# Splitting the input projection weights once and reloading the halves, in a hybrid decoder step on one core

## The chip, the cores and the metric

One core of one Trainium2 chip runs the whole program. The metric is device time in microseconds (us), the median of several runs. Matmuls run on TensorE (PE in the profile, PEld for its weight loads), elementwise work on VectorE (DVE), ScalarE (ACT) and GpSimd (POOL), and almost all transfers are issued from one queue, that of SyncE (SP), which takes its entries in order.

## The reference, cut to what matters

```python
h = rms_norm(x, norm_g)                                   # 2048 prompt tokens and 8 x 4 sample tokens, D = 1024
(sb_q, sb_k, sb_v, sb_g, pl_u, pl_g, gl_q, gl_k, gl_v, gl_g, gl_r, mg) = \
    jnp.split(h @ w_in, _split_points(), axis=-1)          # 9232 columns
o_a = stick_breaking_attention(q, k_all, v_all, ...) * silu(sb_g)     # 8 heads of 64, causal
o_b = multiscale_pool(u_ext, ...) * silu(pl_g)
o_c = rms_norm(gla_chunked(gl_q, gl_k, gl_v, log_a, s0)) * silu(gl_g) # 4 heads, a recurrence in chunks
merged = gates[0] * (o_a @ w_pa) + gates[1] * (o_b @ w_pb) + gates[2] * (o_c @ w_pc)
y = x + merged @ w_o
```

All of it is float32. The change concerns only how the columns of `w_in` reach TensorE.

## The kernel before

**Products from halves.** A float32 product is made of three matmuls of a rounded format (float32r): each operand is split into a high half (the value rounded) and a low half (the value minus the high half), and `mm3` adds high x high, high x low and low x high. So every weight tile is split on the chip: a cast gives `wh` (L160 on DVE or L162 on ACT), a subtraction gives `wl` (L164 on POOL or DVE).

**Groups, phases, units.** The prompt is cut into four groups of 512 tokens (the first also carries the 32 sample tokens). Phase a takes the groups one after the other: the norm, the projections for attention, pooling and the merge gates, and the attention itself. Phase b takes them again for the gated linear attention, four heads per group. Phase c merges the branches and makes the output projection. The weights come in units of 256 columns, each in two halves of the contracted dimension, [128, 4, 256] each, which is 0.5 MiB as float32. A group uses 24 units of `w_in` in phase a and 12 in phase b, so 72 such tiles, and each group loads and splits all of them anew. Phase c has 96 tiles of the other weights.

**The weight pipeline.** `plan` is the list of all weight tiles in the order of use, with the engines that are to split them: cast on DVE and subtraction on POOL in phase a (`SPA`), cast on ACT and subtraction on POOL or DVE by turns (one on POOL, two on DVE) in phase b (`SPB`). `load_h` (L145 to L151) loads the next raw tile into one of two buffers `wr`; `split_h` splits it into one of four buffers `wh` and one of four `wl`. `take`, called at the start of each unit, splits until four tiles stand ready (this unit's two and the next unit's two), then loads raw tiles until six are under way. So a raw tile is loaded two units before its matmuls and split one unit before them. A buffer comes free when the unit that used it is done on TensorE.

**What sets the order.** Matmuls keep their program order (`keep_in_program_order`). The order on the other engines and on the SP queue is chosen when the program is built, by a scheduler that plays the program against a timeline of its own. In phase a the projections of one group are interleaved with the attention of the same group: `z_step` makes scores (`z`), two sigmoids on ACT (L551, L552), a scan on DVE (`om`, L560), a product (`be`, L565, by turns on DVE and POOL); two steps later `t_step` transposes `be` on TensorE and splits the result (`ah` on ACT, L591; `al` on DVE, L592), and `v_step` multiplies these with the values (`acc`). The number of such steps grows with the group: a head takes 2 steps in the first group and 8 in the fourth. In phase b `mix_head` ends each head with a Newton iteration of tiny DVE instructions (`rstd_newton`, L264 to L269, tile `grt`), a product on DVE (`gate`, L1379) and a transpose on TensorE (`z<-ident,gate`). At the start of each group of phase b `h_load` (L292) brings the group's normalised input back from DRAM, as tiles `hTh` and `hTl` of 0.5 MiB for each 128 tokens.

Of the kernel before, what the change touches and what calls it, by code (L numbers as in the profile page):

```python
# [8 lines left out]
F32 = mybir.dt.float32  # L9
F32R = mybir.dt.float32r  # L10
# [7 lines left out]
P = 128  # L18
T = 2048
TG = 512  # L20
NG = T // TG
# [19 lines left out]
NH, PF, PL = 4, 4, 6  # L41
# [28 lines left out]
def f32(ap):  # L70
    return ap.bitcast(F32)
# [3 lines left out]
def hybrid_step(ctx, tc, x_prompt, x_sample, cache_k, cache_v, state_pool, state_gla, page_table, norm_g, w_in,  # L75
                sb_qnorm_g, sb_knorm_g, sb_bias, pool_w, pool_scale, gla_w2, gla_b2, gla_onorm_g, w_pa, w_pb, w_pc, w_o,
                y_p, y_s, k_p, v_p, pool_p, gla_p, k_s, v_s, pool_s, gla_s, phases="abc"):
    nc = tc.nc
# [17 lines left out]
    dram = ctx.enter_context(tc.tile_pool(name="scratch", bufs=1, space=DRAM))  # L96
    wp = ctx.enter_context(tc.tile_pool(name="wp", bufs=1))
# [42 lines left out]

    plan, loaded, ahead = [], [], []
    count = [0]

    def load_h():
        seg, eh, el = plan.pop(0)  # L145
        raw = wp.tile([P, 4, 256], F32, name="wr", bufs=PL - PF)
        o = 0
        for v, n in seg:
            nc.sync.dma_start(raw[:, :, o:o + n], v)
            o += n  # L150
        loaded.append((seg, raw, eh, el))  # L151

    def split_h():
        if not loaded:
            load_h()
        seg, raw, eh, el = loaded.pop(0)
        wl = wp.tile([P, 4, 256], F32R, name="wl", bufs=NH)
        wh = wp.tile([P, 4, 256], F32R, name="wh", bufs=NH)
        if eh[count[0] % len(eh)] == "v":
            nc.vector.tensor_copy(wh, raw)  # L160
        else:
            nc.scalar.copy(wh, raw)  # L162
        count[0] += 1
        (nc.vector if el[count[0] % len(el)] == "v" else nc.gpsimd).tensor_tensor(wl, raw, f32(wh), op=sub)  # L164
        ahead.append((seg, wh, wl))

    def take(*segs):
        n = len(segs)
        while len(ahead) < min(max(n, PF), len(ahead) + len(loaded) + len(plan)):
            split_h()  # L170
        while plan and len(ahead) + len(loaded) < PL:
            load_h()
        got = [ahead.pop(0) for _ in range(n)]
        for (key, _, _), want in zip(got, segs):
            assert [(str(v), m) for v, m in key] == [(str(v), m) for v, m in want]
        return [w[1] for w in got], [w[2] for w in got]
# [4 lines left out]
    def win_unit(cols):  # L181
        return take(*halves(win, cols))
# [7 lines left out]

    def early(n, e):
        for i in range(n):
            plan[i] = (plan[i][0], *e)

    def plan_b():
        us = []
# [94 lines left out]
        for x in range(2):  # L291
            nc.sync.dma_start(f32(HT[x])[:, :, c0:c1], hd[g][x][:, :, c0:c1])  # L292

    # ------------------------------------------------------------------ norm, attention, pooling
    def phase_a(ctx):
        cst = ctx.enter_context(tc.tile_pool(name="cst_a", bufs=1))
        xpool = ctx.enter_context(tc.tile_pool(name="xpool", bufs=1))
# [10 lines left out]
        gB = cst.tile([P, D], F32, name="gB")  # L308
        nc.sync.dma_start(gB, norm_g.broadcast_to([P, D]))
        load_h()  # L310
        nc.sync.dma_start(x0[1], xp[P:2 * P, :])
        load_h()
# [572 lines left out]
            while step():  # L885
                pass

    # ------------------------------------------------------------------ sample attention over the paged cache
    def sample_attn(ctx, cst):
        R = P  # L890
        idv = ident.rearrange("p (b h q) -> p b h q", b=4, h=H)
# [134 lines left out]
            for c in range(4):  # L1026
                nc.sync.dma_start(od[0][c][:, TG + bt * 16:TG + (bt + 1) * 16], og[:, c, :])

    # ------------------------------------------------------------------ gated linear attention
    def phase_b(ctx):  # L1030
        cst = ctx.enter_context(tc.tile_pool(name="cst_b", bufs=1, reuse_waits="tile"))
        gp = ctx.enter_context(tc.tile_pool(name="gla", bufs=1, reuse_waits="tile"))
# [467 lines left out]
        for _ in sa:  # L1500
            n_sa += 1

    # ------------------------------------------------------------------ gates, branch projections, output
    def phase_c(ctx):
        mq = ctx.enter_context(tc.tile_pool(name="mrq", bufs=1, reuse_waits="tile"))
        on = ctx.enter_context(tc.tile_pool(name="on", bufs=1, reuse_waits="tile"))
# [84 lines left out]

    for ph, make in (("a", plan_a), ("b", plan_b), ("c", plan_c)):
        if ph in phases:
            for _ in range(NG):
                plan += make()
    if "a" in phases:
        with ExitStack() as st:
            pin[0] = PIN
            early(2, EARLY)
            banks(st, "pa", **PSA)  # L1600
            phase_a(st)
            pin[0] = False
# [36 lines left out]
```

## Time and profile before

| What | Value |
|---|---|
| median of 3 runs | 3198.27 us (3193.27 to 3203.49) |
| profiled execution, its span | 3195.0 us (3.3 us under the median; the page gives no other time of it) |
| PE busy | 3030.3 us, 95% |
| DVE, ACT, POOL busy | 2225.0 us (70%), 1350.3 us (42%), 1656.2 us (52%) |
| DMA, SP's queue | 417.13 MB, 42.3% of the 16 engines' span |
| first group of phase a | about 0 to 385 us |
| second, third, fourth group of phase a | about 385 to 760, 760 to 1180, 1180 to 1735 us |
| first group of phase b, the other three | about 1735 to 1955, 1955 to 2560 us |
| rest of the last head, and phase c | 2560 to 3195 us |

The busy share of an engine is the time in which it executes something. A busy PE can still be slower than it could be, since matmuls overlap in the pipeline; and an idle engine costs time only if PE, or another engine that PE waits for, waits for it. So the profile is read stage by stage: how busy each engine is in the stage, what PE waits for, and what the instruction that releases PE was itself held up by.

### The profile page before, as it was taken

The numbers are of one execution on the slowest core, as the hardware profiler recorded it, in microseconds if no ns is written. First come the engines' busy times: TensorE is split into PE (matmuls) and PEld (weight loads), VectorE is DVE, ScalarE is ACT, GpSimd is POOL, SyncE is SP. The second block draws the span as 40 slices with busy tenths as digits, with TensorE's granted clock in tenths as the row PEclk, the third lists the DMA queues.
The fourth block names the chain that finished last, engine by engine and source line by source line (L and its number), as shares of the span: only waits on it lengthen the run. The fifth ranks groups of instructions, "written<-read, shape, count | busy, mean of one in ns | idle before, by whom it ended". The sixth has DMA issues, their size and how long they took to land.

```text
span 3195.0 us, 56555 instructions
## 1 busy us (share of the span) xinstructions
PE 3030.3 (95%) x21874; PEld 2654.1 (83%) x21874; DVE 2225.0 (70%) x3968; ACT 1350.3 (42%) x2483; POOL 1656.2 (52%) x1329
## 2 busy tenths in 40 slices
PE   7999999999999999899999999999999989999999
PEld 7899997778877788777778888788878868988999
DVE  7765479777898889998997677757676664443332
ACT  2222324444355453465555544555445543332221
POOL 4555466655756555555544444554545545354442
PEclk9999999999999999999999999999999989999999
DMA  5433454345343444233334344334334337666553
GB/s 191 141 110 120 135 182 136 119 140 188 113 145 111 137 130 149 86 95 88 98 113 144 86 131 139 115 100 142 107 114 129 115 114 243 224 190 205 176 162 113
DMA packets 400960, 437.52 MB, mean 137 GB/s; under 512 B 25968, under 2 KB 323276, under 8 KB 400428
## 3 DMA queue, kind: packets, MB, share of 16 engines
q1 hardware_dynamic: 395572, 417.13, 42.3%
q0 software_dynamic: 5120, 16.78, 1.7%
q8 instruction: 173, 2.83, 0.4%
q14 instruction: 95, 0.78, 0.1%
HBM read 339.22 MB, written 94.78 MB: 136 GB/s over the span
## 4 chain that ended last, share of the span: by engine, by line
PE 39%; DVE 10%; ACT 3%; issue 2%; POOL 1%; DMA 1%; SPq 0%; ACTq 0%; DVEq 0%; POOLq 0%
PE pj L112 21%; PE z L112 13%; DVE om L560 2%; PE at L112 2%; PE acc L112 1%; DVE lv L1094 1%; DVE be L565 1%; PE z L117 1%; PE at L117 1%; DVE grt L268 1%; DVE al L592 1%; DVE gate L1379 0%; DVE lv L1091 0%; PE acc L117 0%; ACT L1121 0%
## 5 line engine op out<-in xcount | busy, mean ns | idle before, releaser
L164 POOL TENSOR_TENSOR wl<-wr,wh 128x1024 fp32r<-128x1024 f32 x272 | 691.8, 2544 | 440.8 <-ACT wh L162 224.5
L112 PE MATMUL pj<-hTh,wh 128*128 128x512 f32 (+2 forms) x1824 | 670.2, 367 | 17.7 <-DVE ut L738 6.3
L112 PE MATMUL pj<-hTh,wl 128*128 128x512 f32 (+2 forms) x1824 | 635.9, 349 | 0.0
L112 PE MATMUL pj<-hTl,wh 128*128 128x512 f32 (+2 forms) x1824 | 635.8, 349 | 0.0
L112 PE MATMUL pj<-wh,hTh 128*128 128x256 f32 (+1 forms) x1840 | 548.4, 298 | 4.0 <-DMA hTh<-hd 2.6
L112 PE MATMUL pj<-wh,hTl 128*128 128x256 f32 (+1 forms) x1840 | 529.2, 288 | 5.3 <-DVE hTl L402 5.3
L112 PE MATMUL pj<-wl,hTh 128*128 128x256 f32 (+1 forms) x1840 | 530.1, 288 | 0.3 <-POOL wl L164 0.3
L112 PEld LDWEIGHTS pj<-hTh,wh 128*128 128x128 f32 x1824 | 348.9, 191 | 80.2 <-issue 27.9
L112 PEld LDWEIGHTS pj<-hTh,wl 128*128 128x128 f32 x1824 | 347.7, 191 | 44.1
L112 PEld LDWEIGHTS pj<-wh,hTh 128*128 128x128 f32 (+1 forms) x1840 | 356.0, 193 | 19.2 <-issue 8.3
L112 PEld LDWEIGHTS pj<-hTl,wh 128*128 128x128 f32 x1824 | 349.5, 192 | 26.9 <-issue 1.0
L565 POOL TENSOR_TENSOR be<-be,om 128x512 f32<-128x512 f32 (+1 forms) x160 | 176.6, 1103 | 364.6 <-DVE om L560 338.6
L112 PEld LDWEIGHTS pj<-wh,hTl 128*128 128x128 f32 (+1 forms) x1840 | 356.4, 194 | 6.2 <-DVE hTl L402 5.9
L112 PEld LDWEIGHTS pj<-wl,hTh 128*128 128x128 f32 (+1 forms) x1840 | 355.6, 193 | 1.4 <-POOL wl L164 0.5
L560 DVE TENSOR_TENSOR_SCAN om<-om,car 128x512 f32<-128x512 f32 x192 | 325.1, 1700 | 28.6 <-ACT om L552 28.2
L162 ACT CAST wh<-wr 128x1024 fp32r<-128x1024 f32 x194 | 202.7, 1048 | 289.8 <-PE pj L112 126.7
L591 ACT CAST ah<-at 128x512 fp32r<-128x512 f32 (+2 forms) x352 | 161.1, 493 | 330.5 <-PE at L117 197.8
L551 ACT ACTIVATE be<-z,bB 128x512 f32<-128x512 f32 (+2 forms) x320 | 200.4, 626 | 237.1 <-DVE z L548 164.3
L160 DVE CAST wh<-wr 128x1024 fp32r<-128x1024 f32 x190 | 201.9, 1064 | 74.1 <-PE pj L112 50.2
L592 DVE TENSOR_TENSOR al<-at,ah 128x512 fp32r<-128x512 f32 (+2 forms) x352 | 189.1, 560 | 72.8 <-ACT ah L591 71.5
L164 DVE TENSOR_TENSOR wl<-wr,wh 128x1024 fp32r<-128x1024 f32 x112 | 149.0, 1332 | 98.3 <-ACT wh L162 95.0
L552 ACT ACTIVATE om<-z,nbB 128x512 f32<-128x512 f32 (+2 forms) x320 | 200.5, 627 | 0.2 <-DVE be L565 0.2
(521 smaller groups left out, 6712.4 us busy)
## 6 DMA issues: line engine op xcount, KB each, us to landing
wr<-in_w_in_dram SPq DMA_DIRECT2D x224, 512.0 KB
wr<-in_w_in_dram SPq DMA_DIRECT2D x128, 256.0 KB
gt<-gd SPq DMA_DIRECT2D x72, 256.0 KB
gd<-gt SPq DMA_DIRECT2D x70, 256.0 KB
wr<-in_w_pc_dram SPq DMA_DIRECT2D x32, 512.0 KB
wr<-in_w_o_dram SPq DMA_DIRECT2D x32, 512.0 KB
x<-in_x_prompt_dram SPq DMA_DIRECT2D x26, 512.0 KB
vc<-vd SPq DMA_DIRECT2D x48, 256.0 KB
```

Source lines behind the costliest of these rows:

```text
L112: i = nc.tensor.matmul(*a, **k)
L117: i = nc.tensor.transpose(*a, **k)
L160: nc.vector.tensor_copy(wh, raw)
L162: nc.scalar.copy(wh, raw)
L164: (nc.vector if el[count[0] % len(el)] == "v" else nc.gpsimd).tensor_tensor(wl, raw, f32(wh), op=sub)
L268: nc.vector.scalar_tensor_tensor(tr, tr, -0.5, xr, op0=mul, op1=mul)
L551: nc.scalar.activation(be[:, :w], z[:, :w], AF.Sigmoid, bias=bB[:, h:h + 1], scale=0.125)
L552: nc.scalar.activation(om[:, :w], z[:, :w], AF.Sigmoid, bias=nbB[:, h:h + 1], scale=-0.125)
L560: nc.vector.tensor_tensor_scan(ov, ov, ov, init, op0=mul, op1=ALU.min)
L565: (nc.vector if i % 2 == 0 else nc.gpsimd).tensor_tensor(be[:, :w], be[:, :w], om[:, 1:w + 1], op=mul)
L591: nc.scalar.copy(ah[:, jr, tr_], pv[:, jr, tr_])
L592: nc.vector.tensor_tensor(al[:, jr, tr_], pv[:, jr, tr_], f32(ah)[:, jr, tr_], op=sub)
```

## The change

In the first group, a tile of `w_in` is loaded raw and split as before, but both halves go into one tile `w2` of [128, 2, 4, 256] (1 MiB, four buffers, in place of four `wh` and four `wl`), and SP stores that tile to a DRAM tile `wk` of its own. In the three later groups the tile is not loaded raw and not split: one transfer of 1 MiB brings `w2` back from `wk`, ready for the matmuls. `load_h` does this, and `take` starts such a load only when fewer than four tiles stand ready or under way, so it is issued one unit ahead of its use, as soon as the buffer is free. Phase c loads and splits as before. Each plan entry carries a key and the word "keep", "load" or "split".

```diff
     def load_h():
-        seg, eh, el = plan.pop(0)
+        seg, eh, el, key, how = plan.pop(0)
+        if how == "load":
+            w = wp.tile([P, 2, 4, 256], F32R, name="w2", bufs=NH)
+            nc.sync.dma_start(f32(w), kept[key])
+            loaded.append((seg, None, w, None, None, how))
+            return
         raw = wp.tile([P, 4, 256], F32, name="wr", bufs=PL - PF)
...
     def split_h():
         if not loaded:
             load_h()
-        seg, raw, eh, el = loaded.pop(0)
-        wl = wp.tile([P, 4, 256], F32R, name="wl", bufs=NH)
-        wh = wp.tile([P, 4, 256], F32R, name="wh", bufs=NH)
+        seg, raw, eh, el, key, how = loaded.pop(0)
+        if how == "load":
+            ahead.append((seg, eh[:, 0], eh[:, 1]))
+            return
+        w = wp.tile([P, 2, 4, 256], F32R, name="w2", bufs=NH)
+        wh, wl = w[:, 0], w[:, 1]
...
+        if how == "keep":
+            kept[key] = dram.tile([P, 2, 4, 256], F32, name=f"wk{len(kept)}")
+            nc.sync.dma_start(kept[key], f32(w))
         ahead.append((seg, wh, wl))
 
     def take(*segs):
...
-        while plan and len(ahead) + len(loaded) < PL:
+        while plan and len(ahead) + len(loaded) < (PL if plan[0][4] != "load" else PF):
             load_h()
...
-            for _ in range(NG):
-                plan += make()
+            for g in range(NG):
+                how = "split" if ph == "c" else "load" if g else "keep"
+                plan += [(seg, eh, el, (ph, i), how) for i, (seg, eh, el) in enumerate(make())]
```

The order of the matmuls is the same in both programs. What else moves is shown at three places, before and after. Line numbers of the changed kernel are 13 to 14 higher from `split_h` on.

POOL, in the fourth group of phase a, where one attention head ends (`oT`) and the next is prepared (`qd`, `kdu`), before:

```order
L565 TENSOR_TENSOR be<-be,om 128x512
L565 TENSOR_TENSOR be<-be,om 128x256
L587 MEMSET ah 128x128
L588 MEMSET al 128x128
L164 TENSOR_TENSOR wl<-wr,wh 128x1024
L565 TENSOR_TENSOR be<-be,om 128x512
L614 TENSOR_TENSOR oT<-oT,sg 64x512
L474 TENSOR_TENSOR qd<-qr__14549,qd 128x4x64
L164 TENSOR_TENSOR wl<-wr,wh 128x1024
L474 TENSOR_TENSOR kdu<-kr__14834,kdu 128x4x64
```

The same place after:

```order
L578 TENSOR_TENSOR be<-be,om 128x512 x2
L578 TENSOR_TENSOR be<-be,om 128x256
L600 MEMSET ah 128x128
L601 MEMSET al 128x128
L578 TENSOR_TENSOR be<-be,om 128x512
L627 TENSOR_TENSOR oT<-oT,sg 64x512
L487 TENSOR_TENSOR qd<-qr__14145,qd 128x4x64
L487 TENSOR_TENSOR kdu<-kr__14422,kdu 128x4x64
```

The subtractions of the weights are gone and the attention's own work follows without them; on DVE the casts are gone in the same way.

SP's queue, at the first units of phase b (`hTh`, `hTl` is the input of 128 tokens, read from `hd`; `gd`, `od` are stores of phase a's last results), before:

```order
L149 DMA wr<-in_w_in_dram 128x4x256
L778 DMA gd_21_299<-gt 128x512
L149 DMA wr<-in_w_in_dram 128x4x256
L778 DMA gd_22_300<-kr__19423 128x512
L616 DMA od_3_193<-oT 128x512
L292 DMA hTl<-hd_1_71 128x8x128
L292 DMA hTh<-hd_0_70 128x8x128
```

The same place after (`w_18859` is a tile `w2`, `wk_18862` its place in DRAM):

```order
L176 DMA wk_18862<-w_18859 128x2048
L155 DMA wr<-in_w_in_dram 128x4x256
L791 DMA gd_21_299<-gt 128x512
L176 DMA wk_18867<-w_18864 128x2048
L155 DMA wr<-in_w_in_dram 128x4x256
L791 DMA gd_22_300<-kr__18873 128x512
L629 DMA od_3_193<-oT 128x512
L305 DMA hTl<-hd_1_71 128x8x128
L305 DMA hTh<-hd_0_70 128x8x128
```

Two stores of 1 MiB now stand ahead of the loads of the third block of tokens.

SP's queue, in the third group of phase a, after the first four heads' queries, keys (`kr`) and values (`vr`) have been projected, before:

```order
L530 DMA kc<-kd_0_78 128x512
L531 DMA kx<-kd_0_78 64x512
L149 DMA wr<-in_w_in_dram 128x4x256 x2
L791 DMA out_dram<-kr__9202 128x4x256
L794 DMA out_dram<-vr__9411 128x4x256
```

The same place after (`w_9219` and `w_9221` are the two tiles of the first four heads' gate unit, `w_9333` and `w_9335` those of the unit after it, the other four heads' queries):

```order
L543 DMA kc<-kd_0_78 128x512
L544 DMA kx<-kd_0_78 64x512
L149 DMA w_9219<-wk_933 128x2048
L149 DMA w_9221<-wk_938 128x2048
L804 DMA out_dram<-kr__9022 128x4x256
L149 DMA w_9333<-wk_1081 128x2048
L149 DMA w_9335<-wk_1086 128x2048
L807 DMA out_dram<-vr__9223 128x4x256
```

The loads for the queries' unit now stand behind the store of the keys, which waits until the keys are normalised on POOL.

## Rows read from the trace of the kernel before

**Rows 1.** The page: its head, and busy time and share of each engine.

```profile
span 3195.0 us, 56555 instructions
PE 3030.3 (95%) x21874; PEld 2654.1 (83%) x21874; DVE 2225.0 (70%) x3968; ACT 1350.3 (42%) x2483; POOL 1656.2 (52%) x1329
```

**Rows 2.** Windows: stretch, length; PE, PEld, DVE, ACT, POOL busy; clock; DMA; GB/s.

```profile
0.00:385.00 385.00, 352.78 (x2692) 339.84 (x2693) 246.04 (x503) 113.87 (x262) 203.77 (x166) 0.97 0.45 140
385.00:760.00 375.00, 368.31 (x2156) 310.40 (x2156) 284.01 (x475) 147.66 (x300) 225.60 (x164) 1.00 0.45 142
760.00:1180.00 420.00, 406.47 (x2395) 337.98 (x2393) 363.79 (x606) 197.55 (x385) 249.01 (x178) 0.99 0.45 138
1180.00:1735.00 555.00, 515.86 (x3032) 418.88 (x3031) 505.51 (x859) 297.19 (x559) 288.76 (x219) 0.97 0.34 104
1735.00:1955.00 220.00, 200.53 (x1924) 187.87 (x1922) 153.24 (x343) 106.17 (x200) 99.17 (x119) 0.97 0.39 114
1955.00:2560.00 605.00, 567.16 (x5553) 502.09 (x5552) 417.90 (x844) 309.16 (x551) 308.53 (x290) 0.97 0.42 124
```

**Rows 3.** Waits of PE, 1180 to 1735: total us, times, longest.

```profile
PE acc L112 <- DVE al L592: 25.5, 24, 3.2
PE at L117 <- ACT kX L507: 5.1, 6, 1.9
```

**Rows 4.** DVE's groups by form, 1180 to 1735: busy us, mean ns; idle before.

```profile
L560 DVE TENSOR_TENSOR_SCAN om<-om,car 128x512 f32<-128x512 f32 x112 | 179.9, 1610 | 17.3 <-ACT om L552 17.1
L565 DVE TENSOR_TENSOR be<-be,om 128x512 f32<-128x512 f32 x56 | 60.5, 1080 | 0.5
L160 DVE CAST wh<-wr 128x1024 fp32r<-128x1024 f32 x46 | 44.7, 973 | 10.4 <-PE pj L112 5.2 <-DMA wr<-in_w_in_dram 5.1
```

**Rows 5.** Instructions of single lines: ns of the shortest/median/longest (L565, L268: whole span).

```profile
L560 DVE TENSOR_TENSOR_SCAN om<-om,car x112: 1251/1279/4279, 1180.2 to 1731.6; 128x512 f32<-128x512 f32 x112
L592 DVE TENSOR_TENSOR al<-at,ah x156: 275/678/692, 1183.9 to 1727.3; 128x512 fp32r<-128x512 f32 x118, 128x256 fp32r<-128x256 f32 x19, 128x128 fp32r<-128x128 f32 x19
L565 DVE TENSOR_TENSOR be<-be,om x160: 255/681/2714, 114.5 to 1731.0; 128x512 f32<-128x512 f32 x96, 128x128 f32<-128x128 f32 x32, 128x384 f32<-128x384 f32 x32
L268 DVE SCALAR_TENSOR_TENSOR grt<-grt,grx x48: 144/163/2293, 1832.3 to 2630.7; 128x4 f32<-128x4 f32 x48
```

**Rows 6.** Timeline in the fourth group of phase a: start us, length us.

```profile
1470.56 2.52 POOL L164 TENSOR_TENSOR wl<-wr,wh 128x1024 fp32r<-128x1024 f32 x1
...
1470.75 3.42 DVE L560 TENSOR_TENSOR_SCAN om<-om 128x512 f32<-128x512 f32 x1
```

**Rows 7.** Waits of PE, 1955 to 2560.

```profile
PE z L117 <- DVE gate L1379: 13.1, 8, 2.9
PE at L112 <- DVE scx L1324: 8.1, 5, 4.2
```

**Rows 8.** Timeline at the end of a head of phase b.

```profile
2334.95 2.39 POOL L164 TENSOR_TENSOR wl<-wr,wh 128x1024 fp32r<-128x1024 f32 x1 [0.34 <-ACT wh L162]
2335.06 2.29 DVE L268 SCALAR_TENSOR_TENSOR grt<-grt,grx 128x4 f32<-128x4 f32 x1
...
2337.58 1.66 DVE L1379 SCALAR_TENSOR_TENSOR gate<-at,gry,gate 128x256 f32<-128x256 f32 x4
```

**Rows 9.** Windows at the starts of the first two groups of phase b.

```profile
1740.00:1750.00 10.00, 10.00 (x86) 10.00 (x86) 4.12 (x5) 3.88 (x7) 1.28 (x1) 1.00 1.00 287
...
1960.00:1970.00 10.00, 10.00 (x88) 9.46 (x87) 8.78 (x31) 2.88 (x7) 1.29 (x1) 1.00 1.02 307
```

**Rows 10.** The chain of work that ended last: start us, us, what.

```profile
1748.24 7.73 DMA hTh<-hd
```

**Rows 11.** Timeline, third group of phase a: PE and SP's queue.

```profile
818.82 0.40 PE L112 MATMUL pj<-hTh,wh 128*128 128x512 f32 x1
...
825.81 0.38 SPq L791 DMA_DIRECT2D out_dram<-kr__9202  x1
...
829.96 0.28 PE L112 MATMUL pj<-wh,hTh 128*128 128x256 f32 x1
```

More of the change, by code (lines that the diff above doesn't have):

```diff
@@ L142, in hybrid_step @@
     count = [0]
+    kept = {}
     def load_h():
-        seg, eh, el = plan.pop(0)
+        seg, eh, el, key, how = plan.pop(0)
[4 more added lines that the diff above has]
+            return
         raw = wp.tile([P, 4, 256], F32, name="wr", bufs=PL - PF)
@@ L150, in load_h @@
             o += n
-        loaded.append((seg, raw, eh, el))
+        loaded.append((seg, raw, eh, el, key, how))
     def split_h():
@@ L168, in take @@
         n = len(segs)
-        while len(ahead) < min(max(n, PF), len(ahead) + len(loaded) + len(plan)):
+        most = len(ahead) + len(loaded) + len(plan)
+        while len(ahead) < min(max(n, PF), most):
             split_h()
-        while plan and len(ahead) + len(loaded) < PL:
+        while plan and len(ahead) + len(loaded) < (PL if plan[0][4] != "load" else PF):
             load_h()
@@ L192, in early @@
         for i in range(n):
-            plan[i] = (plan[i][0], *e)
+            plan[i] = (plan[i][0], *e, *plan[i][3:])
     def plan_b():
```

## The prediction

> **What bounds the kernel now.** I read the busy shares first: PE is busy 95% of the span [rows 1], so nothing is won except where PE is idle, or runs at the lower of its two clock levels. The windows show where that is. In the three groups that the change relieves, PE is idle 6.7, 13.5 and 39.1 us in phase a and 37.8 us in phase b, 97 us in all (length minus PE busy) [rows 2]. The granted clock there is 1.00, 0.99, 0.97 and 0.97 of 2.4 GHz; a mean of 0.97 is some 6% of the time at 1.2 GHz, so a loss of 3% of the stretch: 0, 4, 17 and 18 us, 39 us in all. These two sums, 97 and 39, are all that the change can win on PE.
>
> Then I asked who makes PE wait. In the fourth group of phase a DVE is busy 505.5 of 555 us, 91% [rows 2], and PE waits above all for DVE's `al`, the split of the attention weights: 25.5 of the 39.1 us [rows 3]. In phase b it waits for `gate` and `scx`, both on DVE, 13.1 and 8.1 us [rows 7]. So the second question is what fills DVE, and the third what stretches its instructions. The scan of 512 columns takes 1.28 us in the median, 1.61 in the mean and 4.28 at most [rows 4, 5]. The timeline shows why: a scan that begins 0.2 us after POOL began to subtract a weight tile runs 3.42 us and ends 1.1 us after POOL does, which is most of a scan's own length [rows 6]. In phase b the same is plainer: a DVE instruction on 4 columns (0.16 us in the median [rows 5]) takes 2.29 us and ends with POOL's subtraction to within 0.01 us; `gate`, for which PE waits, follows 0.2 us later [rows 8]. `al`, whose one input lies in PSUM, is never stretched (678 ns in the median, 692 at most) [rows 5].
>
> **What the change removes.** In each later group 48 tiles of phase a lose a cast on DVE and a subtraction on POOL, and 24 tiles of phase b lose a cast on ACT, and a subtraction on POOL or DVE. None of these is on PE; PE's own matmuls are the same, in the same order.
>
> Fourth group of phase a. The casts are 44.7 us of DVE [rows 4]. Scans give back at most 112 x (1.610 - 1.279) = 37 us and the products `be` 56 x (1.080 - 0.681) = 22 us [rows 4, 5]; POOL's other work stretches them too, so I take 45 of these 59. DVE falls from 505 to about 415 us, 75% of the stretch. With a quarter of its time free it no longer runs late by a whole step, and the projections lie two steps ahead of `al`. I take three quarters of the 39 us idle, 29, and half of the clock's 17, 8: **37 us**. Bounds: 0 and 56.
>
> Second and third group. DVE stands at 76% and 87% already [rows 2]; waits are fewer, and some belong to the start of a group, which the change doesn't touch. Half of the 20 us: **10 us**. Bounds: 0 and 24, with the clock's 4.
>
> Phase b, three groups. A tiny instruction held for 2.29 us in place of 0.16 stands just ahead of `gate` [rows 5, 8]; 12 heads times 2.1 us is 25 us, but not every head is hit, while `scx` and the steps before it gain too. Half of the 37.8 us idle, 19, and a third of the clock's 18, 6: **25 us**. Bounds: 0 and 56.
>
> ACT's casts in phase b I cost at nothing: ACT is busy 51% there [rows 2] and PE's waits in these stretches name it for 5 us only [rows 3]. Sum won: **72 us**, between 0 and 136.
>
> **What it adds.** 72 stores of 1 MiB in the first group, and 216 loads of 1 MiB in place of raw loads of 0.5 MiB. When the DMA engines were busy all the time they moved 287 to 307 GB/s [rows 9]; a pair of tiles, 2.10 MB, then takes 6.8 to 7.3 us. That is my price for a unit's load.
>
> Three places matter, since a load is now issued only when its buffers are free, one unit ahead.
> The usual unit: the third group's gate unit runs from 818.82 to 829.96, 11.1 us, back to back [rows 11]. That is the shortest that a load has; on average it is 1350 / 72 = 18.8 us in phase a and 605 / 36 = 16.8 us in phase b [rows 2]. 7.3 us fit in each: cost 0. The running unit is the cover; were it gone, every unit would cost its 7 us.
> Behind another wait: the next unit's loads are queued behind the store of the keys, which SP issued at 825.81, 4.2 us before that unit's first matmul at 829.96 [rows 11]. If that store comes no earlier, the loads begin at about 826 and PE waits 2.7 to 3.2 us, once in this group and less in the others: I take **3 us**, 0 to 10.
> Start of phase b: the DMA engines are saturated, and PE's input `hTh` lands after 7.73 us on the chain that ended last [rows 9, 10]. Two stores of 1 MiB come ahead of it: 0 to 7.3 us, I take **4**, since they wait for splits that may come after the loads. In the next group the weight loads put 1 MiB more ahead of such loads in a full window: **2 us**, 0 to 3.7.
> Queues: SP has 24 entries more in all (72 + 216 added, 264 raw loads gone), some 0.4 us each [rows 11], beside a queue that waits most of the time: 0. In the first group the stores make 131 GB/s on top of 140 in phase a (50.3 MB in 385 us) [rows 2], 271 together; that is nearly full, but the raw loads behind them are due two units later, and nobody waits for the stores until 360 us later. 0, at most 10. A new wait of SP for PE's last unit holds what stands behind it, attention's `kc`, `vc` loads among them; those wait for PE's own steps of about the same time. 0, at most 10.
> Sum lost: **9 us**, 0 to 41.
>
> **The forecast.** 72 - 9 = 63 us less: the execution of 3195.0 us [rows 1] becomes 3132. The median of the runs stands 3.3 us above that span; I carry this over: **3135 us**, 2.0% faster. By about 0.3% a measurement of this kernel can tell two versions apart.
>
> **Rivals.**
> *The relief stops short of PE.* DVE's time is freed, but PE's waits come from the length of the chain scores, sigmoid, scan, product, transpose, not from DVE's load: the wait for `al` becomes one for ACT or for a transpose. For it: 5.1 us of waits are ACT's already [rows 3], and DVE idles 17.1 us for the sigmoid ahead of the scans [rows 4]. Against it: 91% busy. Then only the instructions held directly ahead of `gate` pay, 25 us less the 9 lost: 3182 us, 3170 to 3200. Chance 0.18.
> *All of it comes.* Every wait and every slow stretch of clock goes: 136 - 9 = 127, 3071 us; anything over 100 us belongs here. The waits for ACT speak against it. Chance 0.07. The Trainium skill (Perfetto Trace Analysis, Identifying the Most-Contended Engine) says that matmul busy time is no good measure of what is left on PE, and that weight loads' busy time is; by PEld the four stretches hold 385 us rather than 97. The trace doesn't bear that out here: the unit of 11.1 us above has 48 matmuls end to end, and its loads can't fill it.
> *Loads arrive late (slower).* Place: every unit of the later groups, PE's first matmul of it. The weights double what the DMA engines must bring per unit, and only after a buffer is free. Without its raw loads (25.2 MB in 375 us, 67 GB/s) the second group moves 75 GB/s [rows 2]; of 287 that leaves 212 for the weights, 9.9 us per pair. That is below 11.1, so it holds, but by little; it decides from a pair of 17 to 19 us on, the mean unit. At 20 us a pair the loss is 72 x 1.2 + 36 x 3.2 = 202 us: 3198 - 72 + 202 + 9 = 3337 us. For it: two saturated windows. Against it: 209, 198, 149 and 186 GB/s on average after the change, all under 287. Chance 0.07. The Trainium skill (SBUF — State Buffer, A bandwidth-pool intuition that's wrong) holds that HBM is almost always the bottleneck from end to end; by that rule doubled bytes would cost their time. Its figure of about 358 GB/s for a core gives an estimate of 5.9 us a pair, which would leave this rival no place.
>
> **Chances and range.** Forecast (30 to 100 us won) 0.68, the three rivals 0.18, 0.07, 0.07. The upper end, 3185, takes in a gain of 13 us and so a good half of the first rival; the lower, 3090, a gain of 108. What is left out is the rest of these rivals, about 0.2. Faster by over 0.3% (under 3188.7): 0.68 + 0.07 + 0.11 of the first rival = 0.86. Within 0.3%: 0.07. Slower: 0.07.
>
> **What would show it.** In the profile after: the scan's mean in the fourth group near 1.35 us and DVE near 75% there; PE's idle time there about 10 us; no DVE instruction of 4 columns over 1 us ahead of `gate`; PE busy above 96%. Wrong would be: PE waits named by DMA on `w2` of more than 20 us in total, or DVE at 75% with PE's idle time unchanged.

## The result, and the profile after

The changed kernel takes **3119.3 us** (median of 4 runs, 3117.9 to 3122.0) beside 3198.6 us (4 runs, 3193.3 to 3203.5) for the kernel before on the same chip: a ratio of **0.975**, 95% interval 0.973 to 0.976, or 79 us less. The forecast was 3135 us, the range 3090 to 3185. The sum is near, but three of its terms are far off and a fourth was missing, and their errors cancel; that is what the rest is about.

The head of the page, against [rows 1]: PE has the same 21,874 matmuls in 37 us less, DVE falls from 2225 to 1846 us, POOL from 1656 to 1184.

```profile
span 3117.6 us, 55911 instructions
PE 2992.8 (96%) x21874; PEld 2633.7 (84%) x21874; DVE 1845.9 (59%) x3776; ACT 1283.2 (41%) x2411; POOL 1184.1 (38%) x1161
```

PE's matmuls stand in the same order before and after, but for a few swapped pairs in phase c. So a stage can be cut at the same matmul in both traces, and its lengths compared. These are the windows of the changed kernel, cut where the six of [rows 2] end (columns as there):

```profile
0.00:370.00 370.00, 345.64 (x2691) 332.95 (x2692) 242.00 (x503) 113.88 (x262) 205.88 (x166) 0.99 0.80 278
370.00:744.00 374.00, 368.08 (x2159) 311.91 (x2158) 189.35 (x426) 148.19 (x300) 92.54 (x114) 0.99 0.63 217
744.00:1149.00 405.00, 401.77 (x2397) 336.38 (x2396) 262.12 (x561) 199.68 (x389) 110.98 (x130) 1.00 0.60 205
1149.00:1646.00 497.00, 488.70 (x3029) 403.93 (x3028) 401.22 (x814) 294.87 (x556) 158.83 (x172) 1.00 0.48 164
1646.00:1881.00 235.00, 205.96 (x1928) 192.29 (x1929) 153.57 (x341) 105.68 (x199) 98.96 (x120) 0.93 0.64 215
1881.00:2485.00 604.00, 565.67 (x5573) 501.75 (x5575) 342.50 (x797) 243.70 (x481) 240.49 (x266) 0.98 0.55 185
```

Cut to the exact matmul, the stages changed by (us): first group of phase a **-14.9**, second -1.3, third -15.2, fourth **-58.2**; first group of phase b **+14.9**, the other three together **-0.7**; the rest -2.0; in all -77.4 in the profiled executions. The forecast had 0, -10 (second and third together), -37, +4 and -23 (25 won, 2 lost) in these places, and +3 behind the store of the keys.

**The fourth group of phase a** did what was expected, and more. PE's waits there, against [rows 3]:

```profile
PE acc L112 <- DVE al L605: 3.3, 4, 1.3
PE at L117 <- ACT kX L520: 3.2, 7, 0.7
```

The wait for `al` is down from 25.5 us to 3.3. DVE's groups there, against [rows 4] (line numbers are 13 higher after); the casts are gone, the mean of the scan fell from 1610 to 1362 ns, that of `be` from 1080 to 824:

```profile
L573 DVE TENSOR_TENSOR_SCAN om<-om,car 128x512 f32<-128x512 f32 x111 | 151.0, 1362 | 40.5 <-ACT om L565 40.3
L578 DVE TENSOR_TENSOR be<-be,om 128x512 f32<-128x512 f32 x56 | 46.1, 824 | 0.6
```

Read the last column too: DVE now sits idle 40.5 us ahead of the scans (17.3 before), until ACT's sigmoid is there. It waits for work instead of being late with it.

The 58 us have three parts. 31 are idle time of PE. The other 27 are its busy time (515.9 to 488.7 us), and they are not all the clock's. Matched matmul by matmul, the 130 that began at the lower clock before (34.1 us of the stage) have 33.1 us of the busy time, and 18.8 after: 14 us. The other 13 us are matmuls that began at full clock in both traces, 11 of them `acc`, the product that stood waiting for `al`. One such matmul, before (first two lines) and after:

```profile
1209.34 0.28 PE L112 MATMUL acc<-ah,vc 128*128 128x256 f32 x1
1210.16 0.39 PE L112 MATMUL acc<-al,vc 128*128 128x256 f32 x1 [0.54 <-DVE al L592]
...
1176.60 0.28 PE L112 MATMUL acc<-ah,vc 128*128 128x256 f32 x1
1176.72 0.27 PE L112 MATMUL acc<-al,vc 128*128 128x256 f32 x1
```

After, it begins while the matmul ahead of it still runs and adds some 0.11 us to the busy time. Before, it begins behind 0.54 us of idle time and adds its whole 0.39 us. So here a wait also cost the overlap of the matmul that waited, which no row of idle time shows. (The end of a matmul is modelled in the profile, so how the time splits between idle and busy is rough; their sum is not.)

**Phase b, second to fourth group.** The wait for `gate` is down to 1.3 us (13.1 in [rows 7]), and yet the stage takes 604 us for 605. Waits of PE there:

```profile
PE at L112 <- DVE scx L1337: 11.9, 9, 3.9
PE at L112 <- DVE scq L1261: 7.0, 5, 4.2
PE at L112 <- ACT scx L1336: 6.0, 5, 1.7
...
PE z L117 <- DVE gate L1392: 1.3, 2, 0.8
```

The scores `scx` now take 17.9 us of waits (8.1 before), their diagonal blocks `scq` 7.0, for 1.3 before:

```profile
PE at L112 <- DVE scq L1248: 1.3, 3, 0.6
```

The tiny instructions ahead of `gate` are no longer held for the length of a subtraction: the line that took up to 2293 ns in [rows 5] takes 714 at most. Not all are short, though; a few beside it still take 1.2 to 1.3 us, as some did before.

```profile
L281 DVE SCALAR_TENSOR_TENSOR grt<-grt,grx x48: 144/164/714, 1753.2 to 2552.1; 128x4 f32<-128x4 f32 x48
...
L282 DVE SCALAR_TENSOR_TENSOR gry<-grt,gry x48: 146/163/1283, 1753.4 to 2552.3; 128x4 f32<-128x4 f32 x48
```

**Phase b, first group**, the stage that lost 15 us. Two of its waits grew, that for `hTh` and that for `r`, the decay input. Before (first two lines) and after:

```profile
PE pj L112 <- DMA hTh<-hd: 2.6, 1, 2.6
...
PE z L112 <- DVE r L1107: 0.8, 1, 0.8
...
PE pj L112 <- DMA hTh<-hd: 8.0, 1, 8.0
...
PE z L112 <- DVE r L1120: 4.4, 1, 4.4
```

And a long wait is followed by a slow stretch. In these windows of the same stage PE runs nothing for 5 us with the DMA engines full, while its granted clock falls (0.75 on the mean), and in the next 5 us it is 0.50, the 1.2 GHz level:

```profile
1665.00:1670.00 5.00, 0.00 (x0) 0.00 (x0) 1.21 (x2) 1.53 (x2) 1.16 (x2) 0.75 0.94 291
1670.00:1675.00 5.00, 3.22 (x15) 3.23 (x16) 1.18 (x4) 0.00 (x0) 4.01 (x19) 0.50 1.01 311
```

PE's busy time in the stage rises from 200.5 to 206.0 us for the same work; matched matmul by matmul, 4.4 us of it stand where the clock level differs. 5.4 (hTh) + 3.6 (r) + 5.5 (busy time) = 14.5 of the 14.9 us.

**Weights that come late** there are hardly any. Over the whole span, PE waits for a reload twice, in the second group of phase a:

```profile
PE pj L112 <- DMA w<-wk: 1.9, 2, 1.2
```

### The profile page after: what moved, and what is told of

It is laid out like the page before. It is cut to its first block, busy times and chain, and to the rows that moved or that the text cites. A ratio compares the mean times of both kernels' runs of the same rounds, so it can differ in the third digit from the quotient of the medians.

```text
span 3117.6 us, 55911 instructions
## 1 busy us (share of the span) xinstructions
PE 2992.8 (96%) x21874; PEld 2633.7 (84%) x21874; DVE 1845.9 (59%) x3776; ACT 1283.2 (41%) x2411; POOL 1184.1 (38%) x1161
## 4 chain that ended last, share of the span: by engine, by line
PE 38%; DVE 7%; ACT 3%; DMA 1%; issue 1%; POOL 0%; SPq 0%; DVEq 0%; ACTq 0%; POOLq 0%
PE pj L112 20%; PE z L112 13%; PE at L112 2%; PE acc L112 1%; DVE lv L1107 1%; PE z L117 1%; DVE gate L1392 1%; PE at L117 1%; ACT L1134 0%; DVE lv L1104 0%; DVE Bc L1136 0%; DVE scx L1337 0%; DMA hTl<-hd 0%; ACT lv L1106 0%; DVE grt L280 0%
## 5 line engine op out<-in xcount | busy, mean ns | idle before, releaser
L112 PE MATMUL pj<-hTh,w 128*128 128x512 f32 (+2 forms) x3648 | 1051.9, 355 | 5.9 <-DVE ut L751 3.2
L112 PEld LDWEIGHTS pj<-hTh,w 128*128 128x128 f32 x3648 | 642.2, 188 | 110.5 <-issue 27.7
L112 PE MATMUL pj<-w,hTh 128*128 128x256 f32 (+1 forms) x3680 | 713.4, 293 | 13.5 <-DMA hTh<-hd 8.8
L112 PE MATMUL pj<-hTl,w 128*128 128x512 f32 (+2 forms) x1824 | 630.5, 346 | 0.0
L112 PEld LDWEIGHTS pj<-w,hTh 128*128 128x128 f32 (+1 forms) x3680 | 581.9, 193 | 29.9 <-DMA hTh<-hd 9.2
L112 PE MATMUL pj<-w,hTl 128*128 128x256 f32 (+1 forms) x1840 | 528.8, 287 | 6.0 <-DVE hTl L415 4.2
L112 PEld LDWEIGHTS pj<-hTl,w 128*128 128x128 f32 x1824 | 344.2, 189 | 26.8 <-issue 1.0
L112 PEld LDWEIGHTS pj<-w,hTl 128*128 128x128 f32 (+1 forms) x1840 | 355.9, 193 | 7.2 <-DVE hTl L415 4.7
L173 POOL TENSOR_TENSOR w<-wr,w 128x1024 fp32r<-128x1024 f32 x104 | 256.1, 2464 | 256.8 <-ACT w L171 174.4
L112 PE MATMUL z<-oh,w 128*128 128x512 f32 (+2 forms) x896 | 250.9, 365 | 0.0
L565 ACT ACTIVATE om<-z,nbB 128x512 f32<-128x512 f32 (+2 forms) x320 | 200.1, 625 | 0.0
```

Of the source, the lines that this page charges most:

```text
L112: i = nc.tensor.matmul(*a, **k)
L565: nc.scalar.activation(om[:, :w], z[:, :w], AF.Sigmoid, bias=nbB[:, h:h + 1], scale=-0.125)
```

## The experiments

Twelve kernels ran beside the two. All but e10 and e12 keep PE's order, so that each stage can be set against the kernel before at the same matmuls. Changes of the stages in us, from the traces (g1 to g4 are the four groups; phase b's last three stand together); the ratio to the kernel before is that of the timed runs, with its 95% interval:

| kernel | a g1 | a g2 | a g3 | a g4 | b g1 | b g2-4 | rest | median us | ratio |
|---|---|---|---|---|---|---|---|---|---|
| changed | -14.9 | -1.3 | -15.2 | -58.2 | +14.9 | -0.7 | -2.0 | 3119.3 | 0.975 (0.973-0.976) |
| e1_a_only | -15.1 | -0.8 | -12.4 | -58.2 | +4.7 | -14.5 | -3.0 | 3093.7 | 0.969 (0.968-0.970) |
| e2_b_only | -1.2 | +0.1 | +3.3 | -2.2 | +13.4 | -6.6 | -2.9 | 3198.6 | 1.002 (1.001-1.003) |
| e3_one_tile | -4.2 | +0.2 | +3.4 | +2.2 | +3.1 | -14.6 | -2.6 | 3184.1 | 0.998 (0.997-0.999) |
| e4_defer | -15.3 | -1.5 | -12.9 | -58.2 | +14.1 | -10.5 | -2.7 | 3115.8 | 0.976 (0.975-0.977) |
| e5_no_sub | -1.1 | -7.7 | -14.9 | -51.5 | +5.8 | -0.4 | -3.6 | 3123.2 | 0.979 (0.976-0.981) |
| e6_no_cast | +1.0 | -8.3 | -11.9 | -42.0 | +0.9 | -3.4 | -3.3 | 3128.5 | 0.980 (0.977-0.982) |
| e7_half_loads | -6.2 | -5.6 | -19.0 | -57.8 | +8.2 | -14.6 | -1.6 | 3099.2 | 0.971 (0.968-0.973) |
| e8_store_only | -15.8 | 0.0 | +2.4 | -0.1 | +13.7 | -14.4 | -1.7 | 3178.2 | 0.996 (0.994-0.997) |
| e9_skip6 | -14.4 | -2.1 | -14.7 | -58.2 | +4.1 | -12.4 | -2.4 | 3098.1 | 0.972 (0.970-0.973) |
| e10_x1 | -15.8 | -1.4 | -14.6 | -58.2 | +13.0 | -30.5 | -3.0 | 3086.4 | 0.968 (0.967-0.970) |
| e12_a_x1 | -14.8 | -2.6 | -15.5 | -58.3 | +0.8 | -11.5 | +2.2 | 3098.7 | 0.971 (0.970-0.973) |

Where a group of phase a does the work of the kernel before, its column scatters by up to 4.2 us (e3's first group; 3.4 elsewhere), and the six kernels with the change in phase a as it is lie within 3.1 us of each other; that is the resolution. In phase b it is worse: e4_defer and the changed kernel do the same in its last three groups and differ by 10 us, part of it where PE ran at the lower clock in one and not in the other; and e4_defer's runs reach from 3109.5 to 3120.4 us, of which the profiled one is the fastest. e11_double, at 3516.6 us (ratio 1.103), is told of below and left out of the table. For e10 and e12, whose order in phase b is another, the limits of its stages are approximate. Beside these runs the kernel before took 3188 to 3192 us (medians), 7 to 10 less than in the first comparison; so totals are compared by their ratios, and medians only roughly.

### Which phase the gain is from: e1_a_only, e2_b_only

```
e1:  how = "split" if ph != "a" else "load" if g else "keep"
e2:  how = "split" if ph != "b" else "load" if g else "keep"
```

> Only phase a keeps and reloads its weights; phase b splits in every group as before. Theory 1 (phase b gives back what it wins, its waits moving from the gate to the scores scx, and its first group only pays about 15 us for the two stores ahead of the hT loads): phase a as in the changed kernel (89 us before the old time at its end), nothing lost at the start of phase b, about 3105 us, 14 us under the changed kernel. Theory 2 (the reload in phase b carries its forecast 25 us and the loss at its start comes from elsewhere, from phase a ending earlier): about 3135 to 3145 us.

> Only phase b keeps and reloads its weights; phase a splits in every group as before. Theory 1: phase b wins nothing net and pays some 15 us at its start, so 3199 + 15 = about 3210 us. Theory 2 (25 us won in phase b, 15 lost at its start): about 3189 us.

Measured: 3093.7 and 3198.6 us. e1 goes with theory 1, and beyond it; e2, 0.2% slower than the kernel before beside it, lies between the two numbers and, by that ratio, on theory 1's side. Phase a brings all of the gain; reloading in phase b, as it stands, is worth less than nothing. What theory 1 did not have is that phase b of e1 gains 14.5 us in its later groups although it splits there as before. e3 shows the same without any reload.

### The first group of phase a: e3_one_tile, e8_store_only

```
e3:  how = "split"
e8:  how = "split" if ph == "c" or g else "keep"
```

> Every group splits as before, nothing is stored or reloaded, but the two halves of a weight tile lie in one tile of 1 MiB with one release, as in the changed kernel. Theory 1 (the 14.6 us that the first group of phase a won come from this form, which moves casts and subtractions against the small DVE instructions): the first group ends some 15 us earlier, total near 3184 us or lower. Theory 2 (they come from the stores, or from chance in how the instructions fall): first group within 4 us of before, total near 3199 us.

> The first group of both phases stores its halves as in the changed kernel, but every later group loads the raw weights and splits them as before. Theory 1 (stores cost nothing in the first group of phase a, and 15 us at the start of phase b): the same first group as with one tile and no store, then 15 us lost, so the total is that of the one-tile kernel + 15 us: 3199 us if that one takes 3184. Theory 2 (the stores themselves move the first group's work so that it wins 14.6 us): the first group 15 us ahead here and not there.

e3's median, 3184.1 us, is theory 1's number to the microsecond, and theory 1 is wrong: the first group wins 4.2 us, about theory 2's number, and the gain comes from phase b (-14.6); besides, the kernel before was 7 us faster beside it. A total alone would have settled this the wrong way. e8, which adds the stores to e3 and nothing else, has the first group 15.8 us ahead. So 11 or more of these 15 us come with the *stores*, which were to cost nothing or up to 10 us. (e2's first group does the same work as e3's and wins 1.2 us, so e3's 4.2 may be scatter.) PE's waits in the first group of e3, then of e8:

```profile
PE pj L112 <- DVE ut L751: 5.6, 4, 2.0
...
PE pj L112 <- DVE sg L477: 3.2, 1, 3.2
PE pj L112 <- ACT vr__1613 L444: 3.0, 2, 2.3
```

```profile
PE pj L112 <- DVE ut L751: 3.2, 3, 1.3
...
PE pj L112 <- DVE sg L477: 1.3, 2, 0.9
```

What differs on DVE is where the casts stand. The builder orders DVE, ACT and POOL by a time simulation, and a store that must be read out before a weight tile is free moves the casts: at this place in the first group they now stand behind short steps that PE waits for. DVE in e3 (-) and e8 (+):

```
-CAST W<-wr 128x1024
-CAST W<-wr 128x1024
+TENSOR_TENSOR sg<-sg,pj 128x256
+CAST W<-wr 128x1024
+TENSOR_TENSOR sg<-sg,pj 128x288
 TENSOR_TENSOR sg<-sg,pj 128x256
 TENSOR_TENSOR sg<-sg,pj 128x288
-TENSOR_TENSOR sg<-sg,pj 128x256
-CAST W<-wr 128x1024
-CAST W<-wr 128x1024
-TENSOR_TENSOR sg<-sg,pj 128x288
+CAST W<-wr 128x1024
```

That the 11 us come with the stores is shown. That the order on DVE is how they do it fits the waits, and e7_half_loads (below) speaks for it: it has 48 stores in this group too, of half the size; at this place its order on DVE is that of e3; and its group wins 6.2 us, little more than e3's. As its stores also move half the bytes, this is not a full separation.

### What slowed the later groups of phase a: e5_no_sub, e6_no_cast

Both start from the kernel before (abridged; tiles 48 to 191 are those of the three later groups):

```
e5:  if 48 <= count < 192: cast only; ahead.append((seg, wh, wh))
e6:  if 48 <= count < 192: nc.gpsimd.tensor_tensor(wl, raw, raw, op=add)
                           ahead.append((seg, wl, wl))
```

> The kernel before, but in the second to fourth group of phase a POOL's subtraction is left out and the upper half of the weights is used in both places; the cast on DVE stays, and loads are as before. Theory 1 (what slowed these groups was POOL's subtraction holding DVE's scans and products): most of the 75 us of these three groups comes, 45 to 70 us, total 3130 to 3155 us; scan mean in the fourth group near 1.35 us although the casts stay. Theory 2 (it was the casts' own 45 us on a DVE that is busy 91%): 0 to 20 us, total 3180 to 3199 us.

> The kernel before, but in the second to fourth group of phase a the cast on DVE is left out: POOL makes one tile by adding the raw weights to themselves, an instruction of the same shape and with two inputs as its subtraction, and this tile is used in both places. Theory 1 (POOL's holding of DVE): 0 to 25 us of the 75, total 3174 to 3199 us, scan mean in the fourth group still near 1.6 us. Theory 2 (the casts' load on DVE): 45 to 70 us, total 3130 to 3155 us.

Each run keeps the theory that it was meant for, and so contradicts the other run's: without POOL's subtraction the three groups win 74 us, without DVE's cast 62, and both are gone in the changed kernel, which wins 75. The two do not add; either brings most of it. Window, scan and wait for `al` in the fourth group, of e5:

```profile
1157.00:1661.00 504.00, 492.91 (x3029) 407.23 (x3028) 431.07 (x862) 295.56 (x556) 164.95 (x172) 0.99 0.37 114
...
L564 DVE TENSOR_TENSOR_SCAN om<-om,car 128x512 f32<-128x512 f32 x111 | 150.6, 1360 | 27.1 <-ACT om L556 27.1
...
PE acc L112 <- DVE al L596: 5.6, 6, 1.8
```

and of e6:

```profile
1162.00:1675.00 513.00, 495.30 (x3024) 406.63 (x3023) 447.12 (x816) 295.90 (x557) 252.65 (x218) 0.99 0.37 112
...
L565 DVE TENSOR_TENSOR_SCAN om<-om,car 128x512 f32<-128x512 f32 x111 | 172.6, 1557 | 28.1 <-ACT om L557 27.6
...
PE acc L112 <- DVE al L597: 11.6, 13, 1.9
```

In e6 the scans are still held by POOL (mean 1557 ns) and PE's wait for `al` still falls by half (25.5 to 11.6 us); in e5 the casts are all there (46 of 822 ns) and it falls to 5.6. So neither source alone is the cause. What the four kernels have in order is how much DVE has to do in this stage, from whatever source: 505 us of work before, in 555; 447 in e6, 431 in e5, 401 in the changed kernel, with 0, 42, 52 and 58 us won. The first 58 us taken off DVE are worth 42, the next 46 only 16. That POOL holds the scans is plain in e5, whose scans have the mean of the changed kernel; the Trainium skill (SBUF — State Buffer, Who interferes with whom) states that a DVE instruction with two inputs in SBUF contends with a GpSimd instruction that reads SBUF, and the trace agrees, with 3.42 us for a scan beside a subtraction of 2.52 us [rows 6].

### What the loads cost: e7_half_loads, e11_double

```
e7:  nc.sync.dma_start(f32(w)[:, 0], kept[key]);  the store: nc.sync.dma_start(kept[key], f32(wh))
e11: nc.sync.dma_start(f32(w), kept[key])
     nc.sync.dma_start(again, kept[key])      # a fresh tile in memory
```

> The changed kernel with half the bytes: only the upper half of each tile is stored (0.5 MiB) and reloaded (0.5 MiB), and it is used in both places. Theory 1 (the loads fit beside the running unit): the second to fourth group of phase a and of phase b take the same time as in the changed kernel within 3 us each; only the start of phase b wins, about 7 of its 15 us, total 3110 to 3119 us. Theory 2 (doubled bytes cost time everywhere): 3095 us or less.

> The changed kernel, and behind every reload of 1 MiB the same MiB is copied once more from memory to memory, so that the reloads cost the DMA engines about twice their time; nothing reads the copy. Theory 1 (a unit's loads of 7 us are covered by the running unit, and the cover ends where they take 17 to 19 us): a pair now takes 14 to 19 us, PE begins to wait for weights in the short units, 20 to 100 us in all, total 3140 to 3220 us. Theory 2 (there is more cover than that, since loads need not follow one another): within 10 us of 3119 us.

e7, with half the bytes, is 3099.2 us, between the two numbers. The fourth group of phase a takes the same 497 us; the second and third win 4 us each over the changed kernel, just beyond the scatter of its like, so there the doubled bytes seem to cost something, 8 us in all; the start of phase b wins 6.7 of its 15 us, as expected. Phase b's later groups are 14 us ahead of the changed kernel's, but only 4 of e4_defer's, which load the full tiles: inside that column's scatter.

e11 did not test what it was made for. The copies have no reader, and the builder's order put all 144 of phase a's into the first two groups (133 into the first), and 63 of phase b's 72 into its first; the third and fourth group of phase a move 205 and 164 GB/s, no more than in the changed kernel. Where reloads begin to cost in the later groups stays open. It does show what full DMA engines cost. First group of phase a:

```profile
0.00:642.00 642.00, 408.06 (x2697) 383.40 (x2698) 201.86 (x502) 115.20 (x262) 197.86 (x165) 0.80 0.98 370
```

The share is 0.98 at 370 GB/s, copies from memory to memory among it, the group takes 642 us for 370, and the waits are for weights: the raw loads, behind the copies in SP's queue, reach the cast and the subtraction late.

```profile
PE pj L112 <- DVE w L171: 159.4, 23, 13.6
PE pj L112 <- POOL w L175: 57.1, 32, 4.1
```

### The start of phase b: e4_defer, e9_skip6

```
e4:  if key[0] == "b" and key[1] < 4: late.append(...)   # issued in h_load, after i == 3
e9:  if plan[i][3][0] == "b" and plan[i][3][1] < 6: plan[i] = (*plan[i][:4], "split")
```

> The changed kernel with one difference: the first four stores of phase b are issued behind the last hT load of the group instead of ahead of the first. Theory 1 (these stores, ahead of the hT loads in a full DMA window, are the 14.8 us that the first group of phase b lost): the wait for hTh falls from 8.0 to under 3 us, the total to about 3107 us. Theory 2 (the loss is due to the decay input r, the clock, or to phase a ending earlier): within 4 us of the changed kernel's 3119 us.

> The changed kernel, but the first six weight tiles of a group of phase b are neither stored nor reloaded: every group splits them, as before. Theory 1 (the first group of phase b loses its 15 us because stores of 1 MiB stand between and behind its first loads, of hT, the decay input and the states, while the DMA engines are full): with these six gone the wait for hTh falls from 8.0 to under 4 us, that for r from 4.4 to under 3, the stage takes some 5 us more than before instead of 15, total about 3108 us. Theory 2 (the loss is due to the stores all along the stage, or to phase a ending earlier): within 4 us of the changed kernel's 3119 us.

e4 gave 3115.8 us and +14.1 us in the first group: theory 2's numbers. But it is no test. SP's timeline shows that two of the four stores are still issued between the loads of hT, though the code has them behind the last; the builder orders DMAs too:

```profile
1651.11 2.48 SPq L309 DMA_DIRECT2D hTl<-hd  x1
...
1655.86 0.42 SPq L312 DMA_DIRECT2D wk<-w  x1
...
1656.85 1.23 SPq L312 DMA_DIRECT2D wk<-w  x1
...
1660.22 0.54 SPq L309 DMA_DIRECT2D hTl<-hd  x1
1660.85 5.14 SPq L309 DMA_DIRECT2D hTh<-hd  x1
```

e9 takes the first six stores away (and the reloads of these tiles). The stage is 224 us for 235, its loss +4.1 us, its clock 0.97, and the two waits fall to 1.6 and 2.0:

```profile
1646.00:1870.00 224.00, 201.67 (x1927) 187.87 (x1927) 156.33 (x340) 106.54 (x200) 98.30 (x120) 0.97 0.59 197
...
PE z L112 <- DVE r L1120: 2.0, 1, 2.0
...
PE pj L112 <- DMA hTh<-hd: 1.6, 1, 1.6
```

Theory 1 holds: six stores at this place are 11 of the 15 us, though 18 later ones stay. The 4 us that are left are no more than kernels lose here that store nothing in phase b (e1 +4.7, e3 +3.1). The total, 3098.1, lies below theory 1's number, above all by phase b's later groups (-12.4).

### Why phase b gained nothing: e10_x1, e12_a_x1

```
e10: X1, X2 = 3, 2                 (in the changed kernel)
e12: X1, X2 = 3, 2                 (in e1_a_only)
```

> The changed kernel with X1 = 3 in place of 2: in phase b one more step of projection matmuls stands between the step that asks for the scores and PE's first matmul that reads scx. Theory 1 (in phase b PE now arrives too early at scx, whose chain on DVE and ACT has a length of its own): the waits for scx fall from 17.9 us to under 6 in the second to fourth group, and these take up to 12 us less, total 3107 to 3114 us. Theory 2 (whatever is moved, another wait of the same head takes its place): within 4 us of 3119 us, with new waits of the same sum.

> Reload in phase a only (as in e1_a_only) and X1 = 3 (as in e10_x1): phase b splits its weights in every group, with the later step for scx. Theory 1 (in phase b the reload is worth something once PE no longer stands at scx: the splits hold DVE ahead of the gate, and that wait stays): the second to fourth group of phase b take 585 to 591 us here, 10 to 16 more than with the reload and X1 = 3 (575); at its start this kernel wins some 9 us by having no stores; total 3086 to 3094 us. Theory 2 (X1 = 3 is worth its 30 us whether the weights are split or reloaded, so that the reload in phase b is worth nothing): these groups take 575 us or less, total 3065 to 3078 us.

e10 is the fastest, 3086.4 us, 20 us below the lower end of theory 1's range. Of PE's waits in the last three groups of phase b none is for `scx` any more. The window and what is left of the two others:

```profile
1878.00:2453.00 575.00, 555.19 (x5559) 492.34 (x5557) 337.28 (x797) 242.44 (x480) 239.06 (x265) 0.99 0.57 195
...
PE at L112 <- DVE scq L1261: 1.9, 3, 0.9
PE z L117 <- DVE gate L1392: 1.4, 2, 0.8
```

575 us for 604, 29 less, where 12 were expected at most; 10.5 of them are PE's own busy time, at a clock of 0.99 for 0.98. e12 has the same X1 and splits in phase b:

```profile
1865.00:2458.00 593.00, 561.85 (x5551) 497.55 (x5550) 426.79 (x840) 308.84 (x548) 308.84 (x287) 0.98 0.43 127
...
PE z L117 <- DVE gate L1392: 13.1, 7, 2.9
```

The wait for `gate` is back, 13.1 us, the same sum as in [rows 7], and the stage takes 593 us. So the later step alone is not what helps, nor is the reload alone. With X1 = 2 the split in one tile takes 590 or 591 us (e1, e3, e8), and the reload 604 in the changed kernel, 598 in e2 and 594 in e4 (593 in e9 and 590 in e7, which reload fewer tiles or half the bytes); with X1 = 3 the reload takes 575 and the split 593. Theory 1 holds, with stage and total a little above its numbers: the splits did hold DVE ahead of `gate`, and taking them away let PE arrive early at the next thing of the same head that was not ready. In the five reload kernels with X1 = 2 the waits for `scx` are 18 to 19 us, whatever the stage takes.

## Why the prediction was right, and where it was wrong

**The fourth group of phase a** (37 us forecast, 58 measured). Mechanism and place were right: the wait for `al` fell from 25.5 to 3.3 us, idle time from 39.1 to 8.3, 31 us where 29 were foreseen. What was mis-sized is the term for PE's busy time, 8 us for 27. Of the clock's 17 us, a ceiling that the trace bears out, I took half, and 14 came, as the mean went from 0.97 to 1.00. And 13 us had no term at all: the overlap that a matmul loses when it has waited. The bound of 56 was thereby too low. Further, DVE stands at 81%, not 75%: its 401 us are even fewer than the 415 foreseen, but I had divided by the old length of the stage. And I added the casts and what the scans give back as if each were needed; e5 and e6 show that either brings most of the gain alone.

**The second and third group** (10 forecast, 16.5 measured): right, the third group more than the second, within the bounds.

**Phase b, three later groups** (25 forecast, under 1 measured): this step failed. I had counted that `scx` "and the steps before it gain too", and took half the idle time. The relief at `gate` came nearly in full, 13.1 to 1.3 us; the waits for `scx` and `scq` rose from 9.4 to 24.9. That is the first rival, *the relief stops short of PE*, in this stage though not in the one for which I wrote it. e10 against e12 shows 18 us there for the reload (593 and 575), once PE's order is moved by one step; the other 12 of e10's 30 come without the reload too. The split itself got 14 us faster in one tile (e1, e3, e8): its waits for `gate` and `scx` are 14.0 us for 21.2, and PE's busy time is 6 us less. Why is open. (The 5 us of waits for ACT by which I costed ACT's casts here are those of [rows 3], a stage of phase a; in this one they were 1.3 us before.)

**The start of phase b** (4 forecast, bound 7.3; 14.9 measured): the place was right, and so was the delay of `hTh`, 5.4 us. Not priced were the loads of the decay input behind the same stores, 3.6 us, and PE's longer busy time with the slow stretch after the long wait, 5.5.

**The first group of phase a** (0 forecast, 14.9 won): the step "nobody waits for the stores" was right and incomplete. No wait names them, but the gain comes with them, probably by the order of casts on DVE. I looked at what the stores cost and not at where the split of the first group now stands.

**Behind the store of the keys** (3 forecast): 0. No wait for weights stands in the third or fourth group.

**Sum.** -63 was forecast and -77 came in the profiled execution: -15 (first group) -21 (fourth) -6.5 (second and third) -3 (keys) -2 (rest) +11 (start of phase b) +22 (later groups of phase b). Errors of some 80 us cancelled to 14: that the total came so near is in good part luck. The rival *loads arrive late* is refuted: PE waited 1.9 us for reloads, where over 20 would have been its sign.

## What to carry to other kernels

In the stage where one engine was late all the time, relief of that engine paid from either source, and paid less the more there was of it; price the relief against the slack that is needed, not as a sum of what is taken away. Where PE went from one wait to the next in a short chain (`gate`, then `scx`), removing a wait moved it: look for the next operand that is not ready, and shift PE's order with it. Big stores that nobody waits for moved the time in two ways: the small loads behind them came late, at the start of a phase, and, as far as the runs tell, the builder gave another order to the instructions around them, here for the better.

The reload in both phases with X1 = 3 (3086.4 us; by the ratios, 0.968 to 0.975, 0.7% below the changed kernel) is the best that ran. e9's six tiles without stores, added to it, might take some 9 of the 13 us that its first group of phase b still loses, an estimate from e9's 4.1; that was not tried.

## What the runs showed of the hardware

The DMA engines moved more than the 287 to 307 GB/s on which the price of a load rested [rows 9]: 370 GB/s over the 642 us of e11's first group, at a share of 0.98, part of it copies from memory to memory. By that a pair of tiles, 2.10 MB, would take 5.7 us rather than 7, an estimate.

The price of a wait on PE was not its length. After 5 us without a matmul the clock was at its lower level for the next 5 us (0.50), and PE's busy time in the stage grew by 5.5 us, 4.4 of it with the clock. In the fourth group of phase a, with the waits gone, the reverse was worth 27 us beside the 31 of idle time: 14 at the matmuls that had run at the lower clock, and 13 at full clock, mostly at the `acc` matmuls that had waited, one of which added 0.39 us to the busy time before and 0.11 after.
